# A streamed mixture-of-experts kernel: loads of a skipped branch on another queue, and the last two experts taken one after the other

## The chip, the cores and the metric

The kernel runs on one core of a Trainium2 chip. The metric is the device time of one execution in microseconds (us). An engine is named as the profile names it: PE is the matrix engine, PEld its weight loads, DVE the vector engine, ACT the scalar engine, POOL the GpSimd engine and SP the engine that here does nothing but issue transfers. A "q" behind the name (SPq, ACTq, PEldq) is that engine's instruction queue.

## The reference

One layer of a hybrid encoder over 256 tokens and 16 meta tokens of width 1024: layer norm, an attention branch and a state-space branch, a gated merge, a second norm, and then the part that takes nearly all of the time, a mixture of 32 experts with the best 4 for each token, and a last norm.

```
logits = t @ w_router + b_router
top_v, top_i = lax.top_k(logits, 4);  top_w = softmax(top_v);  comb = scatter(top_w)   # (256, 32)
for e in range(32):
    gate = min(t @ w_gate[e] + b_gate[e], 7)
    up   = clip(t @ w_up[e] + b_up[e], -7, 7)
    act  = (up + 1) * gate * sigmoid(1.702 * gate)
    out  = out + comb[:, e:e+1] * (act @ w_down[e] + b_down[e])
h = layer_norm(2 ** 0.25 * h + out, ln2_g, ln2_b)
```

Every weight matrix is 1024 x 1024 in float32, so an expert has 12 MB of weights and all 32 have 384 MB.

## The kernel before

**Experts in pairs.** The 32 experts are worked off in 16 pairs, p = 0 to 15, of experts 2p and 2p + 1. Up to 64 tokens of each expert (CAP) are gathered by a matrix of zeros and ones (`gather`, which also makes the transposed combine weights `selT` by `weights`). For each expert `gate_up(e)` multiplies the tokens with w_gate and then w_up into the PSUM tiles pg and pu, two halves of the columns side by side in the 128 partitions (matmuls of the form 128*64: 128 rows deep, 64 columns of the array wide). `activate` does the gate function with DVE and ACT, `act_T` transposes the result on PE and copies it back by ACT, `down` multiplies both experts of a pair with w_down into two tiles Yp, which are copied to `Ysb`, and `combine` of the pair before adds the weighted rows to `acc` (four matmuls and four DVE additions), one pair late.

**The ring of slots.** Each weight matrix comes in four transfers of 1 MB (`expert_load`, four "quarters"), 12 for an expert, 24 for a pair. They go into a ring of 20 slots of SBUF in the order that `homes` lays down; one of the slots, gate1, leaves the ring near the end, because a tile gb2 with the gain and the shift of the last norm takes its place (`norm_rows`: 16 matmuls on PE and four ACT copies). All loads are issued by SP in the order of the program; PE and SP run in program order (`manual_schedule`). SP issues a load when the slot has been read and when the load eight places earlier has landed.

**The crowded branch.** If an expert gets more than 64 tokens, the tokens above are worked off by `crowded`, an `If` with a loop over experts inside, that stands between pairs 9 and 10. With this input it is skipped. Ahead of it, the first eight loads of pair 10 (gate and up of expert 20) are issued. The branch's own loads (`weights_of` and two rows of biases) are written for SP, and its tiles take eleven slots, all of the ring but gate1 and those eight.

**The last pair.** In pair 15 `gate_up(31)` has `norm_rows` between the first and the second quarter of w_up. The loads of w_down of experts 30 and 31 come in turns; the last quarter of each is cut in two halves. `down` runs with four matmuls that put `acc` into the PSUM tiles fin (`sums`) ahead of its second and third quarter; then four matmuls add the last combine to fin, and the norm is taken straight from PSUM: mean and variance by DVE (`bn_stats`), a reciprocal root by three Newton steps for each of the two token tiles (`norm_steps`, the two chains interleaved by `steps`), and gain and shift on DVE, ACT and POOL, with three stores on ACT's queue and two on SP's.

Of the kernel before, what the change touches and what calls it, by code (L numbers as in the profile page):

```python
# [9 lines left out]
F32 = mybir.dt.float32  # L10
F32R = mybir.dt.float32r
BF16 = mybir.dt.bfloat16
I32 = mybir.dt.int32
U32 = mybir.dt.uint32
AF = mybir.ActivationFunctionType
ALU = mybir.AluOpType
# [4 lines left out]
P = 128  # L21
# [11 lines left out]
NE = 32  # L33
# [15 lines left out]
def hybrid_trunk_kernel(ctx: ExitStack, tc: tile.TileContext, x, meta, ln_in_g, ln_in_b, w_in, b_f,  # L49
# [650 lines left out]
    def homes():  # L700

        out = list(first)
        while len(out) <= 12 * NE:
            out += [s_ for s_ in slots if s_ != ("keep", "gate1") or len(out) < 12 * NE - 39]
        return out[:12 * NE + 1]

    home = homes()
# [299 lines left out]
    def residual(n):  # L1007
# [3 lines left out]
        for i in range(2):  # L1011
# [3 lines left out]
            V.scalar_tensor_tensor(a, pb_, ALPHA, a, op0=ALU.mult, op1=ALU.add)  # L1015
            V.tensor_add(a, a, r_)

    def weights(p, sel):
        V.tensor_mul(sel, sel, bc(comb[:, :, 2 * p:2 * p + 2], 3, CAP))
        pt = px.tile([P, 512], F32, name="px", tag="px")  # L1020
        for i in range(2):
            TE.transpose(pt[:, i * P:(i + 1) * P], sel[:, i].rearrange("p e s -> p (e s)"), ident)
        selT = mp.tile([P, SEQ], F32, name="selT", tag="selT", bufs=2)
        S.copy(selT, pt[:, :SEQ])
        return selT

    def gather(p):
# [45 lines left out]
        S.copy(aT.rearrange("p j h s -> p (j h s)"), pt)  # L1073
        return aT

    def down(p, aTs, between=None):
        Yp = [py_.tile([P, 512], F32, name="Yp", tag=f"Yp{n}") for n in range(2)]
        for qtr in range(4):
            if between and qtr in (1, 2):
                between(qtr - 1)  # L1080
            wd = [expert_load(w_down, 2 * p + g, qtr) for g in range(2)]
            for k, n in ((0, 0), (0, 1), (1, 0), (1, 1)):
                half, j = qtr // 2, 2 * (qtr % 2) + k
                for g in range(2):
                    TE.matmul(Yp[n][64 * g:64 * g + 64], aTs[g][:, j, half],  # L1085
                              wd[g][:, k, n * 512:n * 512 + 512],
                              start=qtr == 0 and k == 0, stop=qtr == 3 and k == 1, skip_group_check=True)
        V.tensor_copy(Ysb[:, :512], Yp[0])  # L1088
        S.copy(Ysb[:, 512:], Yp[1])  # L1089

    def combine(p, selT):
        for i in range(2):
# [29 lines left out]
    def crowded():  # L1122

        anyc = nc.values_load(cnti[0:1, NE:NE + 1], min_val=0, max_val=SEQ)
        with tc.If(anyc > CAP):
# [16 lines left out]
            with tc.For_i(0, NE, 1) as e:  # L1142
                ce = nc.values_load(cnti[0:1, bass.ds(e, 1)], min_val=0, max_val=SEQ)
                with tc.If(ce > CAP):
                    def weights_of(w, n):
                        ts = []
                        for qtr in range(4):
                            ts.append(slot(n + qtr).rearrange("p (k n) -> p k n", n=D))
                            nc.sync.dma_start(ts[-1], w[0, bass.ds(e, 1), qtr * 256:qtr * 256 + 256]
                                              .rearrange("o (k p) n -> p (o k) n", p=P))  # L1150
                        return ts

                    scr = slot(1)
                    a, sg, br, bu = scr[:, 0:512], scr[:, 512:1024], scr[0:1, 1024:], scr[32:33, 1024:]
                    nc.sync.dma_start(br, b_gate[0, bass.ds(e, 1), :])
                    nc.sync.dma_start(bu, b_up[0, bass.ds(e, 1), :])
                    aT = slot(2).rearrange("p (k t) -> p k t", k=KD)
                    wg_e, wu_e = weights_of(w_gate, 3), weights_of(w_up, 7)
                    for i in range(2):
                        for n in range(2):  # L1160
                            ns = slice(n * 512, n * 512 + 512)
                            pts = []
                            for ws, bb_, r, tag in ((wg_e, br, 0, "pg"), (wu_e, bu, 32, "pu")):
                                pt = pg.tile([P, 512], F32, name=tag, tag=tag)
                                TE.matmul(pt, ones[r:r + 1, 0:P], bb_[:, ns], start=True, stop=False)
                                for k in range(KD):
                                    TE.matmul(pt, h1Td[:, k, i * P:(i + 1) * P], ws[k // 2][:, k % 2, ns],
                                              start=False, stop=k == KD - 1)
                                pts.append(pt)
                            V.tensor_scalar_min(a, pts[0], 7.0)  # L1170
                            S.activation(sg, a, AF.Sigmoid, scale=1.702)
                            V.tensor_mul(sg, sg, a)
                            V.tensor_scalar(a, pts[1], 7.0, -7.0, op0=ALU.min, op1=ALU.max)
                            V.scalar_tensor_tensor(a, a, 1.0, sg, op0=ALU.add, op1=ALU.mult)
                            pt = px.tile([P, 512], F32, name="px", tag="px")
                            for j in range(4):
                                TE.transpose(pt[:, j * P:(j + 1) * P], a[:, j * P:(j + 1) * P], ident)
                            V.tensor_copy(aT[:, 4 * n:4 * n + 4, i * P:(i + 1) * P],
                                          pt.rearrange("p (k t) -> p k t", k=4))
                    wd_e = weights_of(w_down, 7)  # L1180
                    for i in range(2):
                        for n in range(2):
                            ns = slice(n * 512, n * 512 + 512)
                            pt = px.tile([P, 512], F32, name="px", tag="px")
                            for k in range(KD):
                                TE.matmul(pt, aT[:, k, i * P:(i + 1) * P], wd_e[k // 2][:, k % 2, ns],
                                          start=k == 0, stop=k == KD - 1)
                            V.scalar_tensor_tensor(acc[:, i, ns], pt, over[:, i, bass.ds(e, 1)], acc[:, i, ns],
                                                   op0=ALU.mult, op1=ALU.add)

    selT = gather(0)
    prev = None
    for p in range(NE // 2):
        if p == 10:
            for w in (w_gate, w_up):
                for qtr in range(4):
                    ready[w.tensor.name, 2 * p, qtr] = expert_load(w, 2 * p, qtr)
            order.close()
            crowded()
            order.enter_context(tc.manual_schedule(engines={ENG.PE, ENG.SP}))  # L1200
        upA = activate(0, *gate_up(2 * p))
        if p == 5:
            bdown = [load_rows(b_down[0])]
        elif p in (6, 7):
            residual(p - 6)
        elif p in (8, 9):
            down_bias(p - 8)
        if p:
            combine(p - 1, prev)
        upB = activate(1, *gate_up(2 * p + 1, norm_rows if p + 1 == NE // 2 else None))  # L1210
        aA = act_T(upA)
        if p == 0:
            selT = weights(0, selT)
        nxt = gather(p + 1) if p + 1 < NE // 2 else None
        aB = act_T(upB)
        if p + 1 < NE // 2:
            down(p, (aA, aB))
        prev = selT
        selT = nxt
    for qtr in range(3):  # L1220
        for g in range(2):
            e = NE - 2 + g
            ready[w_down.tensor.name, e, qtr] = expert_load(w_down, e, qtr)
    lasts = [expert_load(w_down, NE - 2 + g, 3, load=False) for g in range(2)]
    for k in range(2):
        for g in range(2):
            part_load(lasts[g], w_down, NE - 2 + g, 3, k)
            ready[w_down.tensor.name, NE - 2 + g, 3] = lasts[g]
    order.close()


    with tc.manual_schedule(engines={ENG.PE, ENG.SP, ENG.DVE, ENG.Activation, ENG.Pool}):
        fin = [[pg.tile([P, 512], F32, name=t_, tag=t_) for t_ in ("pg", "pu")] for _ in range(2)]

        def sums(i):
            for n in range(2):
                TE.matmul(fin[i][n], ident, acc[:, i, n * 512:n * 512 + 512], start=True, stop=False)  # L1237

        down(NE // 2 - 1, (aA, aB), sums)
        gm, bt_ = gb2[0][:, 0], gb2[0][:, 1]  # L1240
        res = [norm_tiles() for _ in range(2)]
        gens = [norm_steps(fin[i], res[i]) for i in range(2)]

        def store(i, ns):
            (nc.scalar if i else nc.sync).dma_start(out2[i * P:(i + 1) * P, ns], acc[:, i, ns])
# [15 lines left out]
            G.tensor_mul(acc[:, i, ns], acc[:, i, ns], gm[:, ns])  # L1261
            G.tensor_add(acc[:, i, ns], acc[:, i, ns], bt_[:, ns])

        for i in range(2):
            for n in range(2):
                TE.matmul(fin[i][n], prev[:, i * P:(i + 1) * P], Ysb[:, n * 512:n * 512 + 512], start=False, stop=True)
        steps(6, gens[0])
        steps(1, gens[1])
        steps(2, gens[0])
        steps(4, *gens)  # L1270
        steps(-1, *gens)
        on_pool(0, 512, 1024)
        on_pool(1, 768, 1024)
        centred(0, 0, 512)
# [36 lines left out]
```

## Time and profile before

| | us |
|---|---|
| three runs: lowest, median, highest | 1231.65, 1232.21, 1234.3 |
| the profiled execution | 1234.48 |
| its span from first to last instruction | 1232.8 |
| PE busy | 1128.0 (92%) |
| DVE, ACT, POOL busy | 342.1, 176.5, 70.8 |
| moved by DMA | 433.59 MB, 352 GB/s over the span |

A busy PE is a PE with a matmul in flight, and the ends of matmuls are modelled, so the share says little by itself. The transfers are read from the row of GB/s and from windows of the trace.

### The profile page before, as it was taken

Reading aid. Unit: us, or ns where it says so; the run is one execution under the profiler, and the core shown is the slowest. Engines: PE = TensorE matmul, PEld = TensorE weight load, DVE = VectorE, ACT = ScalarE, POOL = GpSimd, SP = SyncE. Lnnn points to the kernel's source line nnn. Section 1 sums busy time; section 2 is a strip of 40 time slices with the busy share of each in tenths; the row PEclk is TensorE's granted clock in tenths of the full one; section 3 lists DMA queues with packets and bytes.
Section 4 is the critical chain, followed back from the end, with each engine's and each line's share of the span. In section 5 each row is a group of like instructions: output and inputs, shape, how many; then the busy total and the mean of one; then the engine's idle time right before and its main releaser. Section 6 shows DMA issues by size and latency. Waiting matters only on the chain. (4 is left out here: it accounts for less than half of the span.)

```text
span 1232.8 us, 13171 instructions
## 1 busy us (share of the span) xinstructions
PE 1128.0 (92%) x5382; PEld 573.9 (47%) x5383; DVE 342.1 (28%) x789; ACT 176.5 (14%) x385; POOL 70.8 (6%) x118
## 2 busy tenths in 40 slices
PE   4889999998999999999999999898989889999995
PEld 2778788754545444443435343334433333333341
DVE  3968420623121212112131312121212120202023
ACT  2266410311101101010101010101010110101010
POOL 3333200300000000000000000000000000000001
PEclk9999999999999999999999999999999999999998
DMA  7742289557999999999999999999999999999992
GB/s 151 183 111 62 103 212 352 202 217 299 415 420 419 420 419 420 419 418 406 420 419 419 419 419 419 420 419 394 377 419 420 420 420 419 420 419 419 419 419 97
DMA packets 75817, 433.59 MB, mean 352 GB/s; under 512 B 14234, under 2 KB 14586, under 8 KB 26858
## 3 DMA queue, kind: packets, MB, share of 16 engines
q1 hardware_dynamic: 75322, 432.19, 88.7%
q8 instruction: 44, 0.72, 0.2%
q10 hardware_dynamic: 432, 0.52, 0.1%
q14 instruction: 19, 0.16, 0.0%
HBM read 431.64 MB, written 1.05 MB: 351 GB/s over the span
## 5 line engine op out<-in xcount | busy, mean ns | idle before, releaser
L1051 PE MATMUL pu<-w,xy 128*64 128x512 f32 x1024 | 239.0, 596 | 20.9 <-DMA w<-in_w_up_dram 20.9
L1051 PE MATMUL pg<-w,xy 128*64 128x512 f32 x1024 | 238.1, 595 | 5.7 <-DMA w<-in_w_gate_dram 2.9
L1085 PE MATMUL Yp<-w,aT 128*64 128x512 f32 x1024 | 240.8, 603 | 2.2 <-ACT aT L1073 1.5
L1085 PEld LDWEIGHTS Yp<-w,aT 128*64 128x64 f32 x1024 | 98.1, 139 | 131.3 <-issue 115.8
L1051 PEld LDWEIGHTS pu<-w,xy 128*64 128x64 f32 x1024 | 76.6, 136 | 169.0 <-issue 105.5
L1051 PEld LDWEIGHTS pg<-w,xy 128*64 128x64 f32 x1024 | 83.6, 137 | 147.2 <-issue 132.3
L214 PE MATMUL ps<-hT,w 128*128 128x256 f32 (+1 forms) x512 | 121.3, 396 | 2.8 <-ACT pr L595 2.8
L214 PEld LDWEIGHTS ps<-hT,w 128*128 128x128 f32 x512 | 99.3, 196 | 20.3 <-ACT pr L595 3.1
L1061 DVE TENSOR_SCALAR pg<-pg 128x512 f32<-128x512 f32 x32 | 22.4, 699 | 224.0 <-PE pg L1054 224.0
L1062 ACT ACTIVATE ups<-pg 128x512 f32<-128x512 f32 x32 | 19.1, 597 | 435.8 <-DVE pg L1061 435.8
L1088 DVE COPY xy<-Yp 128x512 f32<-128x512 f32 x16 | 11.1, 691 | 240.3 <-PE Yp L1085 240.3
L1064 DVE TENSOR_SCALAR pu<-pu 128x512 f32<-128x512 f32 x32 | 22.4, 699 | 194.9 <-PE pu L1054 194.9
L1096 PE MATMUL px<-xy,selT 128*128 128x512 f32 x120 | 61.8, 636 | 4.7 <-DVE acc L1098 2.6
L945 PE MATMUL px<-sel,z 128*128 128x128 f32 x480 | 59.8, 283 | 0.6 <-DVE sel L950 0.6
L945 PEld LDWEIGHTS px<-sel,z 128*128 128x128 f32 x480 | 58.6, 197 | 0.8 <-ACT aT L1073 0.8
L1261 POOL TENSOR_TENSOR acc<-acc,gb 128x512 f32<-128x512 f32 (+1 forms) x2 | 2.0, 992 | 988.5 <-ACT acc L1259 988.5
L1089 ACT COPY xy<-Yp 128x512 f32<-128x512 f32 x16 | 9.4, 585 | 234.3 <-PE Yp L1085 234.3
L1098 DVE TENSOR_TENSOR acc<-acc,px 128x512 f32<-128x512 f32 x56 | 37.4, 683 | 12.5 <-PE px L1096 12.4
L1096 PEld LDWEIGHTS px<-xy,selT 128*128 128x128 f32 x120 | 20.4, 193 | 42.5 <-DVE acc L1098 19.4
L885 DVE TENSOR_SCALAR xy<-px,pcolP 128x128 f32<-128x128 f32 x60 | 23.7, 410 | 45.5 <-ACT xy L887 43.7
L1073 ACT COPY aT<-px 128x512 f32<-128x512 f32 x32 | 18.7, 586 | 121.7 <-PE px L1071 121.7
L764 PE MATMUL ps<-ya__1272,w 128*128 128x256 f32 x128 | 30.3, 394 | 2.9 <-DVE ya__1272 L809 2.9
(363 smaller groups left out, 807.4 us busy)
## 6 DMA issues: line engine op xcount, KB each, us to landing
w<-in_w_gate_dram SPq DMA_DIRECT2D x128, 1024.0 KB
w<-in_w_up_dram SPq DMA_DIRECT2D x128, 1024.0 KB
w<-in_w_down_dram SPq DMA_DIRECT2D x126, 1024.0 KB
w<-in_w_in_dram SPq DMA_DIRECT2D x16, 1024.0 KB
w<-in_w_o_dram SPq DMA_DIRECT2D x4, 1024.0 KB
w<-in_w_up_a_dram SPq DMA_DIRECT2D x2, 1024.0 KB
w<-in_w_up_b_dram SPq DMA_DIRECT2D x2, 1024.0 KB
w<-in_w_down_dram SPq DMA_DIRECT2D x4, 512.0 KB
```

What stands on the lines that cost most here:

```text
L214: TE.matmul(pt, w[k][:, j * P:(j + 1) * P], hT[:, k, n0:n1], start=k == 0, stop=k == KD - 1)
L764: TE.matmul(pt, w[k][:, d * P:(d + 1) * P], y[:, k], start=k == 0, stop=k == 3)
L885: V.tensor_scalar(out_, in_, g_, b_, op0=ALU.mult, op1=ALU.add)
L945: TE.matmul(pts[k // 4][:, (k % 4) * P:(k % 4 + 1) * P], z1[:, i, paired(k)], sel[:, i].rearrange("p e s -> p (e s)"), start=i == 0 and k ...
L1051: TE.matmul(pt[64 * n:64 * n + 64], XT[:, kk, c0:c0 + CAP], wt[:, k, n * 512:n * 512 + 512], start=kk == 0, stop=False, skip_group_check=True)
L1061: V.tensor_scalar_min(pgt, pgt, 7.0)
L1062: S.activation(up, pgt, AF.Sigmoid, scale=1.702)
L1064: V.tensor_scalar(put, put, 7.0, -7.0, op0=ALU.min, op1=ALU.max)
L1073: S.copy(aT.rearrange("p j h s -> p (j h s)"), pt)
L1085: TE.matmul(Yp[n][64 * g:64 * g + 64], aTs[g][:, j, half], wd[g][:, k, n * 512:n * 512 + 512], start=qtr == 0 and k == 0, stop=qtr == 3 an ...
L1096: TE.matmul(pt, selT[:, i * P:(i + 1) * P], Ysb[:, ns], start=True, stop=True)
L1098: V.tensor_add(acc[:, i, ns], acc[:, i, ns], pt)
```

## The change

There are four parts. The branch's loads are issued by POOL in place of SP. The last pair is done expert by expert: gate, up and down of expert 30, then gate, up and down of expert 31, with the loads in that order; `down_one` puts the two column halves of one expert's result into the two halves of the partitions of one tile, and `combine_one` adds one expert to fin with matmuls that are 64 rows deep (form 64*128), for which `weights` makes a second copy of the combine weights, `selX`, with the halves exchanged. `norm_rows` moves from pair 15 to pair 12, and gate1 leaves the ring earlier. The two Newton chains become one chain on tiles with two columns.

```
-            out += [s_ for s_ in slots if s_ != ("keep", "gate1") or len(out) < 12 * NE - 39]
+            out += [s_ for s_ in slots if s_ != ("keep", "gate1") or len(out) < 9 * NE - 24]
...
 (in weights)
+        if p + 1 == NE // 2:
+            pt = px.tile([P, 512], F32, name="px", tag="px")
+            for i in range(2):
+                for g in range(2):
+                    TE.matmul(pt[64 - 64 * g:128 - 64 * g, i * P:(i + 1) * P], sel[:, i, g], ident,
+                              start=True, stop=True, skip_group_check=True)
+            selX.append(mp.tile([P, SEQ], F32, name="selX"))
+            S.copy(selX[0], pt[:, :SEQ])
...
+    def down_one(e, aT):
+        Y = py_.tile([P, 512], F32, name="Yp", tag=f"Yp{e % 2}")
+        for qtr in range(4):
+            wd = expert_load(w_down, e, qtr)
+            for k in range(2):
+                half, j = qtr // 2, 2 * (qtr % 2) + k
+                for n in range(2):
+                    TE.matmul(Y[64 * n:64 * n + 64], aT[:, j, half], wd[:, k, n * 512:n * 512 + 512],
+                              start=qtr == 0 and k == 0, stop=qtr == 3 and k == 1, skip_group_check=True)
+        return Y
+
+    def combine_one(g, selT, stop):
+        for i in range(2):
+            for n in range(2):
+                c_ = (selT if n == g else selX[0])[64 * n:64 * n + 64, i * P:(i + 1) * P]
+                TE.matmul(fin[i][n], c_, Ysb[64 * n:64 * n + 64, g * 512:g * 512 + 512], start=False, stop=stop,
+                          skip_group_check=True)
...
 (in crowded; the two loads of bias rows likewise)
-                            nc.sync.dma_start(ts[-1], w[0, bass.ds(e, 1), qtr * 256:qtr * 256 + 256]
+                            nc.gpsimd.dma_start(ts[-1], w[0, bass.ds(e, 1), qtr * 256:qtr * 256 + 256]
...
-    for p in range(NE // 2):
+    for p in range(NE // 2 - 1):
...
-        upB = activate(1, *gate_up(2 * p + 1, norm_rows if p + 1 == NE // 2 else None))
+        upB = activate(1, *gate_up(2 * p + 1, norm_rows if p == 12 else None))
...
+    e = NE - 2
+    upA = activate(0, *gate_up(e))
+    combine(NE // 2 - 2, prev)
+    aA = act_T(upA)
+    Y = down_one(e, aA)
+    S.copy(Ysb[:, :512], Y)
+    fin = [[pg.tile([P, 512], F32, name=t_, tag=t_) for t_ in ("pg", "pu")],
+           [px.tile([P, 512], F32, name="px", tag="px"), py_.tile([P, 512], F32, name="Yp", tag="Yp0")]]
+    for i in range(2):
+        for n in range(2):
+            TE.matmul(fin[i][n], ident, acc[:, i, n * 512:n * 512 + 512], start=True, stop=False, skip_group_check=True)
+    upB = activate(1, *gate_up(e + 1, lambda: combine_one(0, selT, False)))
     for qtr in range(3):
+        ready[w_down.tensor.name, e + 1, qtr] = expert_load(w_down, e + 1, qtr)
+    last = expert_load(w_down, e + 1, 3, load=False)
     for k in range(2):
+        part_load(last, w_down, e + 1, 3, k)
+    ready[w_down.tensor.name, e + 1, 3] = last
     order.close()
...
-        down(NE // 2 - 1, (aA, aB), sums)
+        Y = down_one(e + 1, act_T(upB))
+        V.tensor_copy(Ysb[:, 512:768], Y[:, :256])
+        S.copy(Ysb[:, 768:], Y[:, 256:])
+        combine_one(1, selT, True)
...
+        for i in range(2):
+            st = const.tile([P, 2, 6], F32, name="st", tag="st", bufs=3)
+            for c in range(2):
+                V.bn_stats(st[:, c], fin[i][c])
+            V.bn_aggr(mv2[:, i], st)
+        V.tensor_scalar(va2, mv2[:, :, 1], EPS, 0.5, op0=ALU.add, op1=ALU.mult)
+        V.tensor_single_scalar(ti2, va2.bitcast(I32), 1, ALU.logical_shift_right)
+        V.tensor_scalar(rs2.bitcast(I32), ti2, -1.0, float(0x5F3759DF - (1 << 22) - (1 << 31)),
+                        op0=ALU.mult, op1=ALU.add)
+        for _ in range(3):
+            V.tensor_mul(t2, rs2, rs2)
+            V.tensor_mul(t2, t2, va2)
+            V.scalar_tensor_tensor(rs2, t2, -1.5, rs2, op0=ALU.add, op1=ALU.mult)
+        V.scalar_tensor_tensor(nm2, mv2[:, :, 0], -1.0, rs2, op0=ALU.mult, op1=ALU.mult)
...
-        for i in range(2):
-            for n in range(2):
-                TE.matmul(fin[i][n], prev[:, i * P:(i + 1) * P], Ysb[:, n * 512:n * 512 + 512], start=False, stop=True)
-        steps(6, gens[0])
-        steps(1, gens[1])
-        steps(2, gens[0])
-        steps(4, *gens)
-        steps(-1, *gens)
         on_pool(0, 512, 1024)
         on_pool(1, 768, 1024)
```

## Rows read from the trace of the kernel before

**Rows 1.** The page: GB/s in 40 equal slices of the span

```profile
GB/s 151 183 111 62 103 212 352 202 217 299 415 420 419 420 419 420 419 418 406 420 419 419 419 419 419 420 419 394 377 419 420 420 420 419 420 419 419 419 419 97
```

**Rows 2.** Windows: length, five engines' busy us (instructions), PE clock, DMA share, GB/s

```profile
855.00:860.00 5.00, 5.00 (x26) 2.04 (x24) 0.00 (x0) 0.00 (x0) 0.00 (x0) 1.00 0.94 380
860.00:865.00 5.00, 5.00 (x28) 2.08 (x25) 1.39 (x2) 0.60 (x1) 0.00 (x0) 1.00 0.33 136
865.00:870.00 5.00, 5.00 (x23) 1.88 (x20) 0.85 (x2) 0.00 (x0) 0.00 (x0) 1.00 0.86 316
...
925.00:985.00 60.00, 54.61 (x252) 22.08 (x250) 11.16 (x19) 5.04 (x10) 0.00 (x0) 1.00 1.01 420
```

**Rows 3.** Source line 1125, the If: min/median/max ns, first and last start us

```profile
L1125 SPq EVENT_SEMAPHORE  x9: 17/17/17, 844.9 to 864.5; - x9
...
L1125 POOLq EVENT_SEMAPHORE  x1: 17/17/17, 288.1 to 288.1; - x1
...
L1125 PEldq COMPARE_BRANCH  x1: 6207/6207/6207, 848.0 to 848.0; - x1
```

**Rows 4.** Timeline of SP's queue: start us, us, transfers issued

```profile
826.51 7.81 SPq L728 DMA_DIRECT2D w<-in_w_gate_dram  x4
...
864.65 1.97 SPq L728 DMA_DIRECT2D w<-in_w_gate_dram  x4
...
920.93 7.82 SPq L728 DMA_DIRECT2D w<-in_w_up_dram  x4
...
980.79 7.80 SPq L728 DMA_DIRECT2D w<-in_w_up_dram  x4
```

**Rows 5.** Waits of SP, 920 to 1215: us in total, times, longest

```profile
SPq L728 <- PE px L1071: 1.4, 4, 0.4
```

**Rows 6.** Timeline of PE at the end: start us, us, line, count, [idle before]

```profile
1169.33 1.94 PE L1051 MATMUL pu<-w,xy 128*64 128x512 f32 x8 [0.56 <-DMA w<-in_w_up_dram]
...
1171.41 1.98 PE L1096 MATMUL px<-xy,selT 128*128 128x512 f32 x4
...
1175.51 7.09 PE L1051 MATMUL pg<-w,xy 128*64 128x512 f32 x32
...
1184.46 3.88 PE L1003 MATMUL px<-ident,pcol 128*128 128x128 f32 x32
...
1188.28 5.37 PE L1051 MATMUL pu<-w,xy 128*64 128x512 f32 x24
...
1193.80 0.74 PE L1071 MATMUL px<-ident,ups 128*128 128x128 f32 x4
...
1195.27 1.07 PE L1085 MATMUL Yp<-w,aT 128*64 128x512 f32 x2 [0.73 <-ACT aT L1073]
...
1201.33 1.13 PE L1237 MATMUL pg<-acc,ident 128*128 128x512 f32 x2
...
1203.24 3.65 PE L1085 MATMUL Yp<-w,aT 128*64 128x512 f32 x16
...
1208.74 7.09 PE L1085 MATMUL Yp<-w,aT 128*64 128x512 f32 x32
...
1215.79 1.12 PE L1266 MATMUL pg<-xy,selT 128*128 128x512 f32 x2
```

**Rows 7.** Timeline of DVE, POOL and ACT's queue at the end

```profile
1194.64 0.69 DVE L1065 SCALAR_TENSOR_TENSOR ups<-pu,ups 128x512 f32<-128x512 f32 x1
...
1216.95 0.70 DVE L182 BATCH_NORM_STATS2 st<-pg 128x6 f32<-128x512 f32 x1 [1.22 <-PE pg L1266]
...
1222.39 0.22 DVE L172 SCALAR_TENSOR_TENSOR nt<-rs,va 128x1 f32<-128x1 f32 x1
...
1222.75 1.26 POOL L1261 TENSOR_TENSOR acc<-acc,gb 128x512 f32<-128x512 f32 x1 [987.85 <-ACT acc L1259]
1222.84 1.19 DVE L172 SCALAR_TENSOR_TENSOR nt<-rs,va 128x1 f32<-128x1 f32 x1
...
1228.51 1.40 ACTq L1245 DMA_DIRECT2D out_dram<-acc  x3
```

More of the change, by code (lines that the diff above doesn't have):

```diff
@@ L1016, in residual @@
             V.tensor_add(a, a, r_)
+    selX = []
     def weights(p, sel):
@@ L1074, in act_T, with down @@
         return aT
-    def down(p, aTs, between=None):
+    def down(p, aTs):
         Yp = [py_.tile([P, 512], F32, name="Yp", tag=f"Yp{n}") for n in range(2)]
         for qtr in range(4):
-            if between and qtr in (1, 2):
-                between(qtr - 1)
             wd = [expert_load(w_down, 2 * p + g, qtr) for g in range(2)]
@@ L1154, in crowded @@
                     a, sg, br, bu = scr[:, 0:512], scr[:, 512:1024], scr[0:1, 1024:], scr[32:33, 1024:]
[L1155 to L1156 removed]
+                    nc.gpsimd.dma_start(br, b_gate[0, bass.ds(e, 1), :])
+                    nc.gpsimd.dma_start(bu, b_up[0, bass.ds(e, 1), :])
                     aT = slot(2).rearrange("p (k t) -> p k t", k=KD)
@@ L1213, in hybrid_trunk_kernel @@
             selT = weights(0, selT)
-        nxt = gather(p + 1) if p + 1 < NE // 2 else None
+        nxt = gather(p + 1)
         aB = act_T(upB)
-        if p + 1 < NE // 2:
-            down(p, (aA, aB))
+        down(p, (aA, aB))
         prev = selT
         selT = nxt
+    e = NE - 2
[6 more added lines that the diff above has]
+           [px.tile([P, 512], F32, name="px", tag="px"), py_.tile([P, 512], F32, name="Yp", tag="Yp0")]]
@@ L1220, in hybrid_trunk_kernel @@
+    for i in range(2):
+        for n in range(2):
+            TE.matmul(fin[i][n], ident, acc[:, i, n * 512:n * 512 + 512], start=True, stop=False, skip_group_check=True)
+    upB = activate(1, *gate_up(e + 1, lambda: combine_one(0, selT, False)))
     for qtr in range(3):
[L1221 to L1224, printed above, removed]
+        ready[w_down.tensor.name, e + 1, qtr] = expert_load(w_down, e + 1, qtr)
@@ L1225, in hybrid_trunk_kernel @@
+    last = expert_load(w_down, e + 1, 3, load=False)
     for k in range(2):
-        for g in range(2):
-            part_load(lasts[g], w_down, NE - 2 + g, 3, k)
-            ready[w_down.tensor.name, NE - 2 + g, 3] = lasts[g]
+        part_load(last, w_down, e + 1, 3, k)
+    ready[w_down.tensor.name, e + 1, 3] = last
     order.close()
     with tc.manual_schedule(engines={ENG.PE, ENG.SP, ENG.DVE, ENG.Activation, ENG.Pool}):
-        fin = [[pg.tile([P, 512], F32, name=t_, tag=t_) for t_ in ("pg", "pu")] for _ in range(2)]
@@ L1235, in sums @@
-        def sums(i):
-            for n in range(2):
-                TE.matmul(fin[i][n], ident, acc[:, i, n * 512:n * 512 + 512], start=True, stop=False)
-        down(NE // 2 - 1, (aA, aB), sums)
-        gm, bt_ = gb2[0][:, 0], gb2[0][:, 1]
-        res = [norm_tiles() for _ in range(2)]
-        gens = [norm_steps(fin[i], res[i]) for i in range(2)]
+        Y = down_one(e + 1, act_T(upB))
+        V.tensor_copy(Ysb[:, 512:768], Y[:, :256])
+        S.copy(Ysb[:, 768:], Y[:, 256:])
+        combine_one(1, selT, True)
@@ new lines, in hybrid_trunk_kernel @@
+        gm, bt_ = gb2[0][:, 0], gb2[0][:, 1]
+        rs2, nm2, va2 = (const.tile([P, 2], F32, name=t_) for t_ in ("rs2", "nm2", "va2"))
+        mv2 = const.tile([P, 2, 2], F32, name="mv2")
+        res = [(rs2[:, i:i + 1], nm2[:, i:i + 1], mv2[:, i]) for i in range(2)]
+        for i in range(2):
[4 more added lines that the diff above has]
+        V.tensor_scalar(va2, mv2[:, :, 1], EPS, 0.5, op0=ALU.add, op1=ALU.mult)
@@ new lines, in hybrid_trunk_kernel @@
+        ti2 = const.tile([P, 2], I32, name="ti2")
+        t2 = const.tile([P, 2], F32, name="t2")
+        V.tensor_single_scalar(ti2, va2.bitcast(I32), 1, ALU.logical_shift_right)
[5 more added lines that the diff above has]
+            V.scalar_tensor_tensor(rs2, t2, -1.5, rs2, op0=ALU.add, op1=ALU.mult)
@@ L1262, in on_pool @@
             G.tensor_add(acc[:, i, ns], acc[:, i, ns], bt_[:, ns])
-        for i in range(2):
-            for n in range(2):
-                TE.matmul(fin[i][n], prev[:, i * P:(i + 1) * P], Ysb[:, n * 512:n * 512 + 512], start=False, stop=True)
-        steps(6, gens[0])
-        steps(1, gens[1])
-        steps(2, gens[0])
-        steps(4, *gens)
-        steps(-1, *gens)
         on_pool(0, 512, 1024)
```

## The prediction

> **What bounds the kernel now.** I read the page's row of GB/s first [rows 1]. From the eleventh slice to the last but one nearly every slice moves 419 or 420 GB/s: for some 900 us the transfers of the expert weights set the pace. Two slices fall out, 394 and 377, between 832 and 893 us, and the last one holds the end. So there are two places to look at: the dent, and what comes behind the last load.
>
> In the dent the windows show 380, 136 and 316 GB/s over three stretches of 5 us [rows 2]. Against 420 that is (40 + 284 + 104) x 5 / 420 = 5.1 us of transfer lost. The source line of the `If` says why [rows 3]: nine semaphore instructions on SP's queue, the first at 844.9, the last at 864.5 us, and SP's next load is issued at 864.65 [rows 4]. SP has issued the eight loads ahead of the branch and then sits in the skipped branch for 19.6 us, until these eight have landed. POOL, for which no work stands in the branch, passes it with one semaphore instruction at 288.1. The cadence gives the cost a second time: from the load at 920.93 to that at 980.79 there are 24 loads, 2.494 us each. From 826.51 the load 36 places later would be due at 916.3; it is issued at 920.93, 4.6 us late [rows 4]. I take 4.8 us between the two.
>
> At the end I follow PE [rows 6]. At 1169.33 it waits for a load for the last time: up of expert 30 is there. Sixteen loads are to come, 16 x 2.494 = 39.9 us, so the last lands at about 1209.2. PE is never idle for a load again and reaches the last combine at 1215.79, 6.6 us behind the last landing. From 1171.41 the end is bound by PE and then by the norm, not by the transfers. What comes behind 1215.79 is 17.0 us to the end of the span.
>
> **The change part by part.** My sum is made against the profiled execution, whose span is 1232.8 us, with 1.7 us around it. It ran 2.3 us above the median of the three runs, and I take the gain off that median.
>
> *The branch's loads on POOL.* SP has no transfer left in the branch, so it should pass as POOL does now. It doesn't go on at once, though: the branch's tiles stand in eleven slots, which are all that the next loads can have, and their readers in the branch are on PE. So SP waits until PE has left the branch. PE's compare and branch starts at 848.0 and takes 6.2 us, to 854.2 [rows 3]. What is queued behind SP there is the whole stream of loads. At 864.65 the wait cost 4.8 us, one for one, so it is free up to 859.9; 854.2 lies 5.7 us ahead of that, while four of the eight loads are still under way. Value: -4.8, bounds -4.6 and -5.1. POOL has nothing to do between 288 us and the norm, so its own passage costs nothing; without that cover it would delay only the norm's POOL work.
>
> What is late next is PE. Its first load for pair 10 lands at 826.51 + 8 x 2.494 = 846.5, and it starts behind 854.2, 7.8 us late. So far the dent gave most of that back. Afterwards it has to come from PE's idle time, 60 - 54.61 = 5.4 us a pair [rows 2].
>
> *`norm_rows` in pair 12, `selX` in pair 14.* The rows cost PE 3.82 us, from 1184.46 to 1188.28 [rows 6]. In pair 12 they lie under the loads. `selX` is eight matmul instructions of the kind of which 32 take 3.88 [rows 6], 1.0 us, and one ACT copy. Both at nothing as long as PE's idle time holds: 7.8 + 3.8 + 1.0 = 12.6 us are to be made good in pairs 10 to 14, which offer 5 x 5.4 = 27. The ring with 19 slots from about pair 11 on: one slot is 2.5 us of reach, and SP's longest total wait for PE in the last 300 us is 1.4 us [rows 5]. Nothing.
>
> *The last pair.* PE from 1171.41, against before. The norm rows go: -3.82. Down runs as two whole blocks: before, its 64 instructions take 20.5 us from 1195.27 to 1215.79, less two `sums` of 1.91 and one transposition of 1.47, so 15.2; a whole block of 32 takes 7.05 (1208.74 to 1215.79) [rows 6], two 14.1: -1.1. The activation of expert 31 is no longer covered by the transposition of expert 30: PE would stand from 1193.8, where that transposition starts now, to the end of the second DVE operation at 1195.33 [rows 6, 7]: +1.5. The eviction of the last tile is exposed, as both column halves are needed: a copy of 256 columns and two hand-overs, +0.6. `combine_one(0)` is new on this path. The form 64*128 isn't in the trace. Its eight instructions run two at a time if halves of the array work side by side as they do for 128*64 (24 in 5.2 us, 0.217 each [rows 6]): 1.9 with the start. One after the other at the price of the full form (four in 1.91 us [rows 6]) they take 3.8. I take 1.9, as the 128*64 row is the nearer: half an array, two halves on different PSUM tiles. Sum: -3.82 - 1.1 + 1.5 + 0.6 + 1.9 = -0.9. Do the loads come in time? Gate of expert 31 would start at 1175.51 + 1.47 + 7.05 + 3.82 = 1187.9, and its last quarter lands at 1169.33 + 8 x 2.494 = 1189.3, to be used at 1193; the last down block starts near 1207 and needs the final half at 1212, three us after it lands. PE sets the pace.
>
> *The norm.* Before, 17.0 us from the last combine to the end. After: the first statistics start 1.2 behind it [rows 6, 7], four of 0.72, then 15 small operations at 0.2 each [rows 7]: both reciprocal roots at 7.1 us. Then ACT 0.9, POOL 2 x 1.26 + 2 x 0.7 = 4.0, and 3.3 from the last store's issue (1228.51 and two more) to the end [rows 7]: 15.4. But a DVE operation on two SBUF operands that should take 0.2 took 1.19 exactly while POOL's multiplication of 1.26 ran [rows 7]. If the three `shifted` operations (0.74, 0.74, 0.47 by size) take turns with POOL, it is up to 1.6 more, 17.0. I take the blocked end, as that row is the nearer: -0.2, bounds -1.6 and 0. One chain for both tiles gains little, because tile 0 now waits for tile 1 and all POOL work comes late.
>
> Sum: -4.8 - 0.9 - 0.2 = -5.9, span 1226.9, median 1232.2 - 5.9 = **1226.3 us**.
>
> A rule of the Trainium skill (the page Trainium Kernel Development and Optimization, Key Constraints) speaks against the first part: transfers issued from SP, ACT and POOL run on the same 16 DMA engines, and several issuers save only the issue time. By that alone the first term would be nil and the sum -1.1; the rows show a wait of SP and no lack of bandwidth, so they speak for -4.8.
>
> **The rivals.**
>
> *The halves don't run side by side.* `combine_one(0)` costs 1.9 more and the last statistics come 0.4 later: +2.3, 1228.6. For it: no row of the form. Against: the pairs of 128*64.
>
> *The stall stays.* The passage of the branch waits for the eight loads whoever issues the branch's own, or SP's next load waits for POOL's bookkeeping behind them. The sum is -1.1: 1231.1. Against it POOL's and PE's short passages; for it, that only SP now has transfers in the branch, so that no row shows POOL doing it.
>
> *PE becomes the bound (the other side).* If PE can't use its idle time, the 12.6 us above reach the tail, whole: 1226.3 + 12.6 = 1238.9. It delays the end once the slack is under 12.6 / 5 = 2.5 us a pair, and makes the kernel slower by over 0.2% from 12.6 - 8.4 = 4.2 us, that is 0.8 a pair. The row shows 5.4.
>
> *PE leaves the branch later.* Each us behind 859.9 costs one. Another stall of 6.2 us, to 860.4, would cost 0.5; two more, 866.6, give 1233.0. The Trainium skill (Runtime: NRT & Kernel Launch, Instruction fetch mechanics) says that a taken branch out of the fetched window stalls for a fetch; the one long row on PE agrees, no row shows a second.
>
> **How the numbers follow.** The forecast 0.60, with an own range of 1224.5 to 1227.5; the halves 0.16; the stall stays 0.12; PE the bound 0.06; a later exit 0.04; more gained than summed (the norm at -1.6, other terms at their good ends, near 1224) 0.02. The range of 1224.0 to 1229.5 takes in the first two and their bounds and leaves the rest. This kernel's runs spread by 0.2%, 2.5 us, which is what can be told from no change. Faster by more: 0.60 + 0.16 + 0.02 = 0.78; within: 0.12 and half of the later exits, 0.14; slower: 0.08.
>
> **What would show it.** In the profile after: no dent between 855 and 870 us and loads issued again at about 854; SP with few semaphore instructions at the `If`; PE waiting for loads again before pair 15; 3.8 us of `norm_rows` in pair 12; the last combine 0.9 us earlier than 1215.79 less the 4.8; the matmuls of 64 rows two at a time, eight in under 2.2 us; both reciprocal roots 7 us behind it. Wrong would be a gap in the transfers anywhere behind 300 us, PE idle for loads in the last pair, or a tail longer than 17 us.

## The result and the profile after

The changed kernel takes 1223.59 us (median of six runs), the kernel before beside it 1232.9: a ratio of 0.9925 [0.9906, 0.9944]. The forecast was 1226.3 with a range of 1224.0 to 1229.5. The direction and the mechanisms that were named were right. In the profile 2.7 us lie in a place where the prediction had no term at all, and one of its terms came out 1.0 us larger.

The page of the changed kernel, transfers in 40 slices of its span of 1221.0 us, against [rows 1]:

```profile
GB/s 150 187 105 69 104 211 357 221 208 301 413 422 420 423 420 421 422 420 407 421 422 422 421 422 421 421 421 419 422 420 422 421 421 421 421 421 420 422 421 104
```

Two things are to be seen. The dent of 394 and 377 is gone, as forecast. And the other slices moved too: 419 and 420 before, 421 and 422 now, from the eleventh slice on, where no instruction had been touched.

Windows over the place of the former dent, and over the pair in which `norm_rows` now lies (columns as in [rows 2]):

```profile
850.00:855.00 5.00, 5.00 (x26) 1.90 (x23) 0.00 (x0) 0.00 (x0) 0.00 (x0) 1.00 1.01 416
855.00:860.00 5.00, 5.00 (x28) 2.13 (x26) 1.39 (x2) 0.60 (x1) 0.00 (x0) 1.00 1.02 419
860.00:865.00 5.00, 4.80 (x19) 1.73 (x16) 2.45 (x4) 0.00 (x0) 0.00 (x0) 1.00 1.01 421
...
985.00:1045.00 60.00, 58.25 (x285) 26.36 (x283) 11.42 (x20) 7.39 (x14) 0.00 (x0) 0.97 1.01 421
```

The source line of the `If`, now line 1153, against [rows 3]:

```profile
L1153 POOLq EVENT_SEMAPHORE  x5: 17/43/43, 285.5 to 285.9; - x5
...
L1153 SPq EVENT_SEMAPHORE  x1: 17/17/17, 839.6 to 839.6; - x1
L1153 PEldq COMPARE_BRANCH  x1: 6067/6067/6067, 841.5 to 841.5; - x1
```

SP passes with one semaphore instruction instead of nine; the bookkeeping went to POOL, which does it at 286 us. SP's waits from 830 to 870 us say what holds it instead:

```profile
SPq L728 <- PEq L1153: 6.3, 1, 6.3
...
SPq L1153 <- SPq L1153: 0.2, 1, 0.2
```

It waits 6.3 us for PE to leave the branch, as the prediction had it. SP's timeline, against [rows 4]:

```profile
285.90 3.76 SPq L728 DMA_DIRECT2D w<-in_w_down_dram  x3
...
821.54 7.79 SPq L728 DMA_DIRECT2D w<-in_w_gate_dram  x4
831.53 7.79 SPq L728 DMA_DIRECT2D w<-in_w_up_dram  x4
847.76 1.77 SPq L728 DMA_DIRECT2D w<-in_w_gate_dram  x4
...
891.78 7.77 SPq L728 DMA_DIRECT2D w<-in_w_up_dram  x4
...
911.66 2.80 SPq L728 DMA_DIRECT2D w<-in_w_up_dram  x2
```

PE at the end, against [rows 6]:

```profile
1159.42 1.94 PE L1062 MATMUL pu<-w,xy 128*64 128x512 f32 x8 [0.55 <-DMA w<-in_w_up_dram]
...
1186.66 0.69 PE L1116 MATMUL pg<-xy,selT 64*128 64x512 f32 x1
1186.67 0.69 PE L1116 MATMUL pu<-xy,selX 64*128 64x512 f32 x1
...
1188.58 5.37 PE L1062 MATMUL pu<-w,xy 128*64 128x512 f32 x24
...
1195.68 0.74 PE L1082 MATMUL px<-ident,ups 128*128 128x128 f32 x4 [1.52 <-DVE ups L1076]
1197.16 7.09 PE L1108 MATMUL Yp<-w,aT 128*64 128x512 f32 x32 [0.73 <-ACT aT L1084]
1205.23 0.69 PE L1116 MATMUL pg<-xy,selX 64*128 64x512 f32 x1 [0.99 <-ACT xy L1273]
```

The matmuls of 64 rows start in pairs, 0.01 us apart: all eight of `combine_one(0)` take 1.92 us (1186.66 to 1188.58).

The two executions, cut at the same instructions:

```
stretch                                            before    after   difference
start to the first loads (w_down, pair 0)          288.77   285.90     -2.9
from there to the first load of expert 20          537.74   535.64     -2.1
from there, 36 loads on (the dent lies here)        94.42    90.12     -4.3
from there to PE's last wait for a load            248.40   247.76     -0.6
from there to the first matmul of the last combine  46.46    45.81     -0.65
from there to the end of the span                   17.0     15.8      -1.2
```

The first row belongs to no kernel: the instructions ahead of it stand in the same order, and it begins at 286.2 to 291.3 us in the executions of the experiments, with and without the change (289.2 in the kernel before run again, 291.3 in the changed kernel with the six small tiles moved). Without it the sum is -8.9, beside -9.3 in the medians. The forecast's own terms stand in rows three, five and six: 4.3 + 0.65 + 1.2 = 6.2, where 5.9 was forecast. Rows two and four, -2.7 together, are the ones without a term.

### The profile page after: what moved, and what is told of

Read it like the earlier page. It is cut to its first block, busy times and chain, and to the rows that moved or that the text cites. A ratio compares the mean times of both kernels' runs of the same rounds, so it can differ in the third digit from the quotient of the medians.

```text
span 1221.0 us, 13200 instructions
## 1 busy us (share of the span) xinstructions
PE 1124.1 (92%) x5398; PEld 588.9 (48%) x5399; DVE 340.4 (28%) x782; ACT 177.3 (15%) x387; POOL 71.6 (6%) x118
## 4 chain that ended last, share of the span: by engine, by line
DMA 53%; PE 38%; DVE 5%; ACT 1%; issue 1%; POOL 1%; SPq 1%; POOLq 0%; ACTq 0%; DVEq 0%
DMA w<-in_w_up_dram 29%; DMA w<-in_w_down_dram 16%; PE ps L214 7%; PE pu L1062 6%; PE pg L1062 6%; PE Yp L1094 5%; DMA w<-in_w_gate_dram 5%; PE ps L764 2%; PE px L945 2%; DMA w<-in_b_down_dram 2%; PE Yp L1108 1%; PE ps L936 1%; PE po L936 1%; PE px L1124 1%; DMA prow<-in_ssm_a_im_dram 1%
## 5 line engine op out<-in xcount | busy, mean ns | idle before, releaser
L1094 PE MATMUL Yp<-w,aT 128*64 128x512 f32 x960 | 228.1, 611 | 0.0
L1094 PEld LDWEIGHTS Yp<-w,aT 128*64 128x64 f32 x960 | 101.5, 141 | 114.7 <-issue 99.1
L1062 PEld LDWEIGHTS pu<-w,xy 128*64 128x64 f32 x1024 | 81.4, 136 | 154.8 <-issue 108.9
L1062 PEld LDWEIGHTS pg<-w,xy 128*64 128x64 f32 x1024 | 86.6, 137 | 140.4 <-issue 134.0
L887 ACT ACTIVATE xy<-px,pcolP 128x128 f32<-128x128 f32 x60 | 25.8, 455 | 44.6 <-PE px L945 42.6
```

What stands on the lines that cost most here:

```text
L887: S.activation(out_, in_, AF.Identity, scale=g_, bias=b_)
L1062: TE.matmul(pt[64 * n:64 * n + 64], XT[:, kk, c0:c0 + CAP], wt[:, k, n * 512:n * 512 + 512], start=kk == 0, stop=False, skip_group_check=True)
L1094: TE.matmul(Yp[n][64 * g:64 * g + 64], aTs[g][:, j, half], wd[g][:, k, n * 512:n * 512 + 512], start=qtr == 0 and k == 0, stop=qtr == 3 an ...
```

## The experiments

### The branch's loads and the tail, each alone

The kernel before, run again unchanged, says what a comparison can tell.

> The kernel before, unchanged, against itself. The changed kernel gained 9.3 us in the medians where the prediction's terms sum to 5.9. Theory one, the surplus is the spread of executions (the granted clock in the front, the rate of the transfers): this run's median may differ from the other's by 1 to 3 us in either direction, with an interval of about 0.2% each way around 1.000. Theory two, the surplus belongs to a part of the change: this run agrees with its own kernel within 1 us, and the surplus has to show in one of the runs of a part.

Measured: 1232.67 us, 0.9996 [0.9983, 1.001]; span 1233.0, the stretch to expert 20 537.5. That is 1.0 us from the 1233.64 beside it, so the spread alone doesn't give the surplus of 3 us: it has to be looked for in the parts.

*The kernel before, with only the branch's loads moved* (all three places):

```
-    nc.sync.dma_start(...)      # weights_of, br, bu
+    nc.gpsimd.dma_start(...)
```

> The kernel before with only the branch's loads on POOL. Sum of the terms: the dent of 4.3 to 4.8 us goes, 1228 us, ratio 0.9961 to 0.9965; nothing in the windows between 850 and 870 us below 410 GB/s; the last pair ends as before, PE 6 to 7 us behind the last load. Rival, the dent is worth more than the profile of before shows, since the whole surplus is here: 7.5 us, ratio 0.994. Rival, the branch's passage costs the same from POOL: ratio 1.000.

Measured: 1228.35 us, 0.996 [0.9948, 0.9972], by that ratio 4.9 us less (4.3 and 5.3 against the two medians of the kernel before beside it, 1232.67 and 1233.64). SP has one semaphore instruction at the `If` and issues loads again at 849.45:

```profile
L1125 SPq EVENT_SEMAPHORE  x1: 17/17/17, 841.7 to 841.7; - x1
```

The windows from 850 to 865 us show 410, 416 and 419 GB/s, and the other slices are still at 418 to 421. This part gives what was forecast for it and nothing else.

*The changed kernel, with the branch's loads back on SP* (the same edit the other way):

> The changed kernel with the branch's loads back on SP, so that the last pair, the norm rows and the one Newton chain are left. Sum of the terms as the profile after has them (0.65 us of PE's chain in the last pair, 1.2 us behind the last combine): -1.9 us, ratio 0.9985, the dent at 850 to 870 us back with 4 to 5 us. Rival, the surplus of 3 us is in the tail: -4.5 to -5 us, ratio 0.996. The time from the last load that PE waits for (up of expert 30, last quarter) to the end of the span: 61.5 us by the first, 58.5 by the rival.

Measured: 1227.74 us, 0.9959 [0.9945, 0.9974]. The dent is back (401 and 371 in the page's slices), and SP's waits from 830 to 870 us show the old stall:

```profile
SPq L1153 <- SPq L1153: 19.3, 2, 18.9
```

So the rest of the change is worth about 5 us where the forecast had 1.1. At the end it shows only 0.6 and 1.4 (1163.75 to 1209.58 on PE, then 15.6). The missing 3 us have to lie in the stream: it takes 535.8 us to expert 20, as in the changed kernel, and SP still stalls.

*The changed kernel, with two of the fourteen loads of the branch left on SP*: `br` and `bu`; the other twelve are quarters of weights.

```
-    nc.gpsimd.dma_start(br, ...); nc.gpsimd.dma_start(bu, ...)
+    nc.sync.dma_start(br, ...);   nc.sync.dma_start(bu, ...)
```

> The changed kernel with the two loads of bias rows of the skipped branch left on SP, the weights' on POOL. Theory, SP waits in the skipped branch only for those earlier loads whose semaphores the branch's own transfers would use next, which are the oldest ones: 2 loads, 3 semaphore instructions on SP, the wait over when the second of the eight has landed, some 2 to 5 us behind the branch, before PE leaves the branch; no dent, time as the changed kernel within 1 us. Rival, any transfer of SP in the branch makes SP wait for all eight: the dent of 4.3 us is back, ratio 0.996 where the changed kernel has 0.9925.

Measured: 1225.94 us, 0.9937 [0.992, 0.9955]. The median is 2.4 us above the changed kernel's, more than the 1 us expected, but the intervals overlap, and the profiled execution (span 1221.4, against 1221.0) is the fastest of six; so the trace decides and not the time. The row of the `If`, and then SP's waits from 830 to 870 us:

```profile
L1153 SPq EVENT_SEMAPHORE  x3: 17/17/17, 840.8 to 845.2; - x3
```

```profile
SPq L1153 <- SPq L1153: 4.5, 3, 2.5
SPq L728 <- PEq L1153: 1.3, 1, 1.3
```

Three semaphore instructions instead of nine or one, 4.5 us instead of 19.3 or 0.2, and all of it under PE's own passage: SP goes on at 848.97, and the windows around it show no dent (419, 411, 423). With two of the branch's loads left on SP the stall is short, with all of them it is long.

*The changed kernel, with the branch's loads on ACT* (`nc.gpsimd` to `nc.scalar` in the three places).

> The changed kernel with the skipped branch's loads issued by ACT in place of POOL. Theory from the run with two loads left on SP: an engine waits in the skipped branch for the earlier transfers whose semaphores the branch's own would use. If ACT's transfers use the same eight semaphores as SP's, ACT waits there for SP's eight loads and SP's next load waits for ACT: the dent of 4 to 5 us is back and ACT leaves the branch some 20 us later than the 830.7 of the changed kernel; ratio 0.996. If each queue has its own, ACT passes at once, as POOL does: no dent, 0.9925.

Measured: 1228.87 us, 0.9958 [0.9937, 0.9979]. The dent is back (402 and 370 in the page's slices), but by another engine's wait than had been looked for. The source line of the `If`:

```profile
L1153 SPq EVENT_SEMAPHORE  x9: 17/17/17, 840.5 to 860.3; - x9
L1153 ACTq EVENT_SEMAPHORE  x2: 17/17/17, 831.6 to 831.7; - x2
```

and SP's waits from 830 to 870 us:

```profile
SPq L1153 <- SPq L1153: 19.5, 2, 19.3
```

It is SP that waits, for loads which ACT would issue; ACT itself passes at once. What frees SP is therefore not that another engine issues these loads, but that POOL does.

The built programs say why. In them every load has a semaphore that it raises; loads of SP and of ACT take turns on the same eight (DMAHW0 to DMAHW7), loads of POOL on eight others (DMASW0 to DMASW7). The path for a branch that is not taken raises each semaphore as the branch's loads would have done, and waits first until it stands where the loads ahead of the branch leave it. In the kernel before and in `act_branch` SP does this for all eight, which are those of its eight loads in flight; in `two_left` for those of the two oldest of them (DMAHW1 and DMAHW2); in the changed kernel for none, and POOL's eight have nothing in flight. With one more for its own order that makes the 9, 9, 3 and 1 semaphore instructions of SP in the traces.

### Where the ring of slots lies

The stream had become faster in `tail_only`, but not in `pool_only`. Of what `tail_only` has, one thing reaches all the stream: the one Newton chain has six new constant tiles (`rs2`, `nm2`, `va2`, `mv2`, `ti2`, `t2`). Each takes 32 bytes of a partition, and 6 x 32 = 192 bytes is how far the addresses of the built program move the ring's first slot. Eighteen of the slots follow one another from there, 8 KB each; nine in ten of the loads of expert weights go through them, and the places below are theirs. Of the other two, gate1 moved as far but lies by itself (28192 in the kernel before), and fk's, at 216544, didn't move in any of these kernels. Where the expectations say "every slot but fk's", it is these eighteen.

*The kernel before, with 192 bytes of padding* and nothing of the change:

```
-    warm = const.tile([P, 1], F32, name="warm")
+    warm = const.tile([P, 56], F32, name="warm")     # only column 0 is used
```

> The kernel before, with one small constant tile made 192 bytes larger in each partition, so that every slot of the ring but fk's starts where the changed kernel's do (56480 in place of 56288 bytes into the partition for the first one), and nothing else. Found in the traces so far: in all three kernels with the new last pair the loads move at 421 to 422 GB/s, in all three without it at 419 to 420, from the start of the stream on; from the load at the start of the stream (first quarter of gate behind the first pair's down) to the first load of expert 20 is 537.5 us in the one kind and 535.7 in the other. The instructions in that stretch are the same; what differs is six small tiles of the norm, 192 bytes. Theory, the place of the slots sets the rate: 1.8 us less in that stretch, 2.6 us over the whole stream, ratio 0.9979. Rival, the rate comes with something else of the changed program: 537.5 us and ratio 1.000.

Measured: 1230.84 us, 0.9972 [0.9956, 0.9988]. The page's slices stand at 420 to 422 outside the dent, which stays (388, 384). SP's timeline gives 822.90 - 287.24 = 535.7 us to expert 20:

```profile
287.24 3.76 SPq L728 DMA_DIRECT2D w<-in_w_down_dram  x3
...
822.90 7.85 SPq L728 DMA_DIRECT2D w<-in_w_gate_dram  x4
```

*The changed kernel, with the six tiles in the pool `mp`*, so that the slots lie as before:

```
-    rs2, nm2, va2 = (const.tile([P, 2], F32, name=t_) ...)     # mv2, ti2, t2 too
+    rs2, nm2, va2 = (mp.tile([P, 2], F32, name=t_) ...)
```

> The changed kernel with the six small tiles of the norm taken from another pool, so that the ring's slots start where those of the kernel before do. Theory, the place sets the rate: 537.5 us in the stretch from the first loads of the stream to the first load of expert 20, 419 to 420 GB/s, and 2.6 us more than the changed kernel: ratio 0.9946 where the changed kernel has 0.9925. Rival: 535.7 us, ratio 0.9925.

Measured: 1228.43 us, 0.9947 [0.9927, 0.9966]. The slices are back at 419 and 420, the stretch takes 538.3 us, the tail from the first matmul of the last combine is still 1229.4 - 1213.63 = 15.8:

```profile
1213.63 0.69 PE L1116 MATMUL pg<-xy,selX 64*128 64x512 f32 x1 [0.99 <-ACT xy L1273]
```

So the place of the slots is a cause by itself. The remaining four runs ask which place is good. `after_pad32` and `after_256` are the changed kernel with `warm` of 16 and 32 columns; `after_512` is `after_mp` and `before_512` the kernel before, each with 16 (a wider `warm` takes 32 bytes more with 16 columns, 96 with 32).

> As the kernel with the tiles in another pool, and the small constant tile 32 bytes larger, so that every slot but fk's starts at a multiple of 512 bytes (56320). If the rate depends on how a row of 8 KB falls on boundaries of 512 or 256 bytes, this is the best place there is: as fast as the changed kernel's or faster by 1 to 3 us, ratio 0.990 to 0.9925. If only the 192 bytes as such count, or a boundary that is not among these: as the kernel with the tiles in another pool, 0.9946.

> The changed kernel with the small constant tile 32 bytes larger: slots at 56512, a multiple of 64 bytes but not of 256 or 512. If a boundary of 64 bytes counts, the rate is above the 421 to 422 GB/s of the changed kernel and as in the kernel at multiples of 512; if it is the boundary of 256 or 512, it is as the changed kernel's or between the two; if place doesn't matter, 0.9925 as well.

> The kernel before with the small constant tile 32 bytes larger, so that every slot of the ring but fk's starts at a multiple of 512 bytes, and nothing else. Theory, the place of the slots sets the rate of the loads whatever the kernel does with them: 426 to 427 GB/s from the start of the stream, 530 us from its first loads to the first load of expert 20 in place of 537.5, a load every 2.457 us in place of 2.494, and 13 to 14 us less in all, ratio 0.989. Rival, the gain of the run at multiples of 512 bytes came together with the changed last pair: 3 us or less, ratio 0.9975 or above.

> The changed kernel with the small constant tile 96 bytes larger: slots at 56576, a multiple of 256 bytes and not of 512. If 256 bytes are the boundary that counts, the rate is 426 to 427 GB/s and the time as in the run at multiples of 512, 1213 us, ratio 0.983. If it is 512, the rate is between 421 and 424 GB/s and the ratio 0.988 to 0.993.

Measured (the first slot's byte from the build, the stretch from SP's timeline, GB/s by windows of 120 us in the middle of the stream):

```
kernel          first slot   behind 256 B  stretch to   GB/s        time, ratio to before
                             boundary by   expert 20
before            56288        224          537.7        420
after_mp          56288        224          538.3        420        1228.43  0.9947 [0.9927, 0.9966]
before_pad192     56480        160          535.7        421        1230.84  0.9972 [0.9956, 0.9988]
changed kernel    56480        160          535.6        421        1223.59  0.9925 [0.9906, 0.9944]
after_pad32       56512        192          535.5        421, 422   1222.99  0.9921 [0.9893, 0.9949]
before_512        56320          0          529.0        427        1217.86  0.9865 [0.9841, 0.989]
after_512         56320          0          529.9        427        1213.26  0.9832 [0.9805, 0.9859]
after_256         56576          0          530.7        427        1214.67  0.983 [0.9805, 0.9854]
```

56512 is a multiple of 64 bytes and gains nothing over 56480; 56576 is a multiple of 256 but not of 512 and gains as much as 56320. So a multiple of 64 isn't enough, and one of 256 is. Whether 128 would do isn't shown: no kernel had these slots at a multiple of 128 that is not one of 256. The gain was larger than expected: `after_512` is 10.3 us below the changed kernel, for 1 to 3, and `before_512` 16.8 below the kernel before, for 13 to 14. The page of `before_512` shows it with the dent still in it:

```profile
GB/s 150 188 98 77 105 201 358 217 219 279 411 426 427 427 427 426 427 425 419 427 426 427 427 427 427 425 428 406 379 427 427 427 427 425 427 427 427 427 426 91
```

and the timeline of SP in `after_512`, 904.89 - 885.27 for eight loads, 2.453 us each instead of 2.494:

```profile
286.66 3.76 SPq L728 DMA_DIRECT2D w<-in_w_down_dram  x3
...
885.27 7.63 SPq L728 DMA_DIRECT2D w<-in_w_up_dram  x4
...
904.89 4.29 SPq L728 DMA_DIRECT2D w<-in_w_up_dram  x2
```

Some 350 of the 386 loads go through these slots. 32 bytes of padding in the kernel before are worth 16.8 us (1234.66 to 1217.86), more than the whole change, and with the change 1213.26 us beats both kernels.

The Trainium skill (DMA: Bandwidth & Descriptors, How a descriptor splits into AXI transactions) says that a transfer whose descriptor does not begin at a 256 byte boundary has a first transaction that begins at the boundary below. The runs fit that boundary, without showing that it is this one. That page of the Trainium skill counts bytes that are fetched, and here it is the destination that moves; an estimate by its count, with a descriptor for each 8 KB row, is 263 beats instead of 256 for a row that begins 224 bytes behind the boundary, 262 for 192 and 261 for 160, which is 2.7, 2.3 and 2.0% more. Measured by the load, 224 costs 1.7% and 160 costs 1.3% (2.494 and 2.485 against 2.453), and 192 is no worse than 160: the sizes are not those of the estimate, and the mechanism stays open.

### The norm

*The changed kernel with two Newton chains*, interleaved as before, in place of the one for both tiles:

```
-    V.tensor_scalar(va2, mv2[:, :, 1], EPS, 0.5, ...)     # and the rest of the one chain
+    gens = [norm_steps(fin[i], res[i]) for i in range(2)]
...
+    steps(6, gens[0]); steps(1, gens[1]); steps(2, gens[0]); steps(4, *gens); steps(-1, *gens)
```

> The changed kernel with the two interleaved Newton chains of the kernel before; as the six small tiles are gone too, its slots start where those of the kernel before do, so its whole time compares with the changed kernel with the tiles in another pool (ratio 0.9947). What is looked at is the tail from the last combine's first matmul to the end of the span, 15.8 us in the changed kernel and 17.0 in the kernel before. If the one chain gained it: 17.0 again. If it is the pairwise combine that makes all four parts ready sooner, and the chain itself gains nothing: 15.3 to 16.0, since the first tile's root is then ready earlier and POOL starts earlier.

Measured: 1229.38 us, 0.9957 [0.9941, 0.9972]. Its six tiles are gone, so its slots lie as before (stretch 537.5), and it is to be held against `after_mp`: 1.0 us more, intervals that overlap, so the profile decides. From the first matmul of the last combine to the end it takes 1230.0 - 1213.03 = 17.0 us; `after_mp` 15.8. The other traces agree: 16.8 to 17.2 us in the six with two chains, 15.5 to 15.8 in the eight with one. The timeline of PE, DVE and POOL says why:

```profile
1213.03 0.69 PE L1116 MATMUL pg<-xy,selX 64*128 64x512 f32 x1 [0.99 <-ACT xy L1273]
...
1219.73 1.26 POOL L1296 TENSOR_TENSOR acc<-acc,gb 128x512 f32<-128x512 f32 x1 [985.23 <-ACT acc L1294]
...
1219.82 1.19 DVE L172 SCALAR_TENSOR_TENSOR nt<-rs,va 128x1 f32<-128x1 f32 x1
...
1221.24 1.11 DVE L186 SCALAR_TENSOR_TENSOR nm<-mv,rs 128x1 f32<-128x1 f32 x1
```

Tile 0's early POOL work blocks two small steps of tile 1's chain, for 1.19 and 1.11 us where such steps take 0.22 and 0.16.

## Why the prediction was wrong, and where it was right

**The step that failed** is the one that made the transfers' pace a constant: "for some 900 us the transfers of the expert weights set the pace", and every cost was then worked out at 420 GB/s and 2.494 us a load. The change looked as if it touched the stream only at the branch. It also pushed all slots but one 192 bytes on, and the pace went to 421 and 422: -2.7 us in the profile, shown alone by `before_pad192` and taken back by `after_mp`. Nothing in the trace of before shows it; the addresses of the two programs would have shown the move, though not what it is worth. The prediction gave 0.02 to more being gained than its sum, and looked for that in the sizes of its own terms.

**The term that was mis-sized** is the norm. Of bounds of -1.6 and 0 the value -0.2 was taken, next to the blocked end (which by the prediction's own numbers is 0), because "tile 0 now waits for tile 1 and all POOL work comes late". Measured: -1.2 (17.0 to 15.8), and 17.0 again with two chains. Both roots are ready 6.7 us behind the last combine (7.1 forecast), and DVE does take turns with POOL afterwards. The timeline of DVE, POOL and ACT's queue of the changed kernel:

```profile
1211.73 0.16 DVE L1294 SCALAR_TENSOR_TENSOR nm<-mv,rs 128x2 f32<-128x2 f32 x1
...
1212.84 1.26 POOL L1313 TENSOR_TENSOR acc<-acc,gb 128x512 f32<-128x512 f32 x1 [979.58 <-ACT acc L1311]
...
1213.13 1.52 DVE L1306 SCALAR_TENSOR_TENSOR acc<-acc,rs,gb 128x512 f32<-128x512 f32 x1
...
1214.18 1.59 POOL L1314 TENSOR_TENSOR acc<-acc,gb 128x512 f32<-128x512 f32 x1
...
1216.35 1.78 ACTq L1297 DMA_DIRECT2D out_dram<-acc  x3
```

One `shifted` step grew from 0.74 to 1.52 and one POOL step from 1.26 to 1.59. That costs half of the 1.6 us that were added for it: from the roots to the end it is 9.1 us, where the sum without turns has 15.4 - 7.1 = 8.3. What the step overlooked is that [rows 7] show this blocking in the kernel before, inside its Newton steps, and that a single chain with POOL idle is rid of it there.

**The branch** was right: -4.8 forecast, -4.3 in the profile and 4.9 in `pool_only`. SP waits for PE's exit, PE's passage is the one long one (6.07 us), and no second appears. Only why SP passes was put too simply, "SP has no transfer left in the branch": in `act_branch` it has none either and waits 19.5 us. What counts is whose semaphores the branch's loads would raise, as the built programs above show. The rule quoted against this part (the Trainium skill, Trainium Kernel Development and Optimization, Key Constraints) holds for the bandwidth: `pool_only` moves the same 418 to 421 GB/s. The gain was a wait of SP's queue, which is neither bandwidth nor issue time.

**PE after the branch** makes the delay good, as forecast: from 850 to 1160 us it waits for `up` loads 22 times again, 11.6 us in total, with `norm_rows` in the stretch from 985 to 1045 us (58.25 us busy of 60). The rival of PE as the bound falls.

**The last pair** gives -0.65 for -0.9. The halves run side by side (1.92 us for 1.9), the activation is exposed by 1.52 for 1.5, the two down blocks take 7.1 each. The eviction is 1.0 us instead of 0.6: the copies by DVE and ACT were meant to overlap, yet ACT's waits for DVE's, as the same timeline shows a little earlier:

```profile
1204.29 0.42 DVE L1272 COPY xy<-Yp 128x256 f32<-128x256 f32 x1 [8.66 <-PE Yp L1108]
...
1204.81 0.37 ACT L1273 COPY xy<-Yp 128x256 f32<-128x256 f32 x1 [7.70 <-DVE xy L1272]
```

**The sum.** Against the 1232.9 us beside the result the forecast of 5.9 would have been 1227.0. Of the 3.4 us beyond it the profile shows 2.7 of pace and 1.0 of the norm, less 0.75 by which the branch and the last pair gave less than forecast; the rest, under half a us, is within what two sets of runs of one kernel differ by (1.0).

## What to carry to other kernels

Where a stream of transfers sets the pace, look at the addresses of its buffers first, and try them on 256 byte boundaries before tuning the order of the work; a few small tiles allocated ahead of a ring move all of it and can hide or fake the gain of an edit. Compare two versions only with their buffers at the same place behind such a boundary. And look at the source line of a branch that is not taken: a queue can wait there for transfers that have nothing to do with it, and the semaphores in the built program say which.

## What the runs showed of the hardware

- The place of the 8 KB slots in SBUF sets the pace of the loads into them: 427 GB/s with eighteen of the twenty on a 256 byte boundary, 421 to 422 at 160 or 192 bytes behind one, 419 to 420 at 224. Why 192 is not between 160 and 224 stays open, and other offsets, 128 among them, weren't tried.
- With the loads of a skipped branch on ACT, SP waits for 19.5 us and ACT for nothing; with them on POOL SP waits for 0.2 us.
- DVE steps on a column (128x1) take 1.19 and 1.11 us instead of 0.22 and 0.16 while POOL works on 128x512.
- The matmuls of 64 rows on two halves of the array start 0.01 us apart, and eight take 1.92 us with the change of form on both sides.
- The first load starts anywhere from 286 to 291 us in executions whose front is the same. What sets that wasn't looked into.
